# Attention scores QK^T on one core: two-bank PSUM tiles, copies shared by ScalarE and VectorE, and operands kept by half blocks

## The chip, the cores and the metric

The kernel runs on one core of one Trainium2 chip. The time of a kernel is the device time of one execution in microseconds, and several executions are summed up by their median. One more execution is taken by the hardware profiler; everything said about engines, waits and transfers comes from that one.

## What is computed

```python
def setup_inputs():
    batch, n_heads, seq, head_dim = 8, 12, 1024, 64
    return {
        "q": np.random.randn(batch, n_heads, seq, head_dim).astype(np.float32) * 0.1,
        "k": np.random.randn(batch, n_heads, seq, head_dim).astype(np.float32) * 0.1,
    }

def reference(q, k):
    return np.einsum('bhid,bhjd->bhij', q, k).astype(np.float32)
```

There are 96 independent heads. Each multiplies a 1024x64 matrix by the transpose of another one and gives 1024x1024 float32 scores, 4 MiB. All inputs together are 50.3 MB and the output is 402.7 MB.

## The kernel before

**Blocks.** The 96 heads are cut into blocks of 2, 2, 4 and then eleven blocks of 8 (`sizes`, line 33). A block's Q and K are loaded as float32 by one transfer each (`load`, line 70; the first two blocks head by head, line 82), cast to float16 by GpSimd, transposed so that the head dimension of 64 lies along the partitions, and multiplied by TensorE.

**From input to operand.** For all blocks but the first two, `cast_quads` (line 117) issues four GpSimd casts per half tile (line 131), each of 32 partitions by 1024 elements. `transpose_quads` (line 143) then has VectorE transpose 32x32 squares of a half tile (line 149). It writes with a gap: the view `"c (i r) -> c r i"` puts neighbouring elements of one square 64 elements, 128 bytes, apart for a block of 8. In return the result lies in the order of the rows of the head. A block's Q and K stay in one tile each of 4096 columns (`alloc`, line 139, two buffers). The first two blocks go through TensorE transposes instead (`transpose_rows`, line 151).

**Pairs.** In the blocks of 8, two heads share one pass over TensorE. `space` (line 194) spreads Q into one of two constant tiles, `spaced_even` and `spaced_odd`, of which every second column is zero for each half of the partitions (VectorE copies, line 200, two for a pair). `pair_scores` (line 208) then runs eight steps; each fills a PSUM tile of four banks (128x2048 float32) with four matmuls (line 219), and ScalarE copies the tile to the output tile `o_sb` in SBUF (line 226). Two PSUM tiles rotate. A pair's output tile is 128 partitions by 16384 float32, 8 MiB, and one transfer from the SP queue writes it to DRAM (line 233). Two output tiles rotate, so the copies into a tile wait for the transfer that last read it.

**Order.** Every instruction keeps program order on its engine (`pin`). Work for the next block is put between the steps of a pair by the dictionary `side`: after step 0 the `space` of the next pair, after step 1 the transposes of the next block, and in the third pair of a block, after steps 2 and 6, the two loads of the block after next (issued from ScalarE's queue, line 77). GpSimd's casts follow a queue of their own (`to_half`, line 274). The heads of the first three blocks are written singly, into halves of the two output tiles (`scores`, line 160); head 0 is copied in 1024-element pieces by ScalarE and VectorE in turn.

Of the kernel before, what the change touches and what calls it, by code (L numbers as in the profile page):

```python
# [13 lines left out]
def kernel(  # L14
# [11 lines left out]
    GMAX = 4  # L26
    assert D == 64 and NT == 8 and BH % (2 * GMAX) == 0

# [4 lines left out]
    sizes = [2, 2, 4] + [8] * ((BH - 8) // 8)  # L33
    assert sum(sizes) == BH
    PE_BLOCKS = 2
    NMAX = max(sizes)
    SINGLES = 3
    CHUNK = 32 * 32
# [8 lines left out]
    half_pool = ctx.enter_context(tc.tile_pool(name="half_pool", bufs=3))  # L47
    tr_pool = ctx.enter_context(tc.tile_pool(name="tr_pool", bufs=2))
    out_pool = ctx.enter_context(tc.tile_pool(name="out_pool", bufs=2))

    pin = tc.keep_in_program_order

    def half_tile():
        half_sb = half_pool.tile([P, CHUNK], F16, tag="half")
        return half_sb

    class Block:

        def __init__(self, first, N, by_pe):
            self.first, self.N, self.by_pe = first, N, by_pe
            self.R = N * S // P
            self.elems = self.R * D
            self.raw = [None] * 2
            self.rows = [None] * 2
            self.halves = {}
            self.cut = max(1, self.R * 32 // CHUNK + (self.R * 32 % CHUNK > 0))

        def load(self, x, eng):  # L70
            if self.raw[x] is None:
                x_sb = in_pool.tile([P, self.elems], F32, tag="x")
                self.raw[x] = x_sb
            start = self.first * S
            src = (qf, kf)[x][start : start + self.N * S]
            pin(
                eng.dma_start(
                    out=self.raw[x], in_=src.rearrange("(p r) d -> p (r d)", p=P)
                )
            )  # L80

        def load_head(self, n, x, eng):

            start = (self.first + n) * S
            src = (qf, kf)[x][start : start + S]
            m = S * D // P
            pin(
                eng.dma_start(
                    out=self.raw[x][:, n * m : (n + 1) * m],
                    in_=src.rearrange("(p r) d -> p (r d)", p=P),  # L90
                )
            )

        def cast_rows(self, x):
            n = S * D // P
            self.rows[x] = half_tile()[:, : 2 * n].rearrange(
                "p (r h d) -> p r h d", h=2, d=D
            )
            for half in range(2):
                pin(  # L100
                    nc.gpsimd.tensor_copy(  # L101
                        out=self.rows[x][:, :, half],
                        in_=self.raw[x][:, half * n : (half + 1) * n].rearrange(
                            "p (r d) -> p r d", d=D
                        ),
                    )
                )

        def chunks(self):
            return [  # L110
                (x, part, c)
                for x in range(2)
                for part in range(2)
                for c in range(self.cut)
            ]

        def cast_quads(self, x, part, c):

            m = self.R // self.cut
            half_sb = half_tile()[:, : m * 32]
            self.halves[x, part, c] = half_sb
            raw = self.raw[x].rearrange("p (r h d) -> p r h d", h=2, d=32)
            for half in range(2):
                b = 2 * half + part
                for h in range(2):
                    q0 = 32 * (2 * half + h)
                    pin(  # L130
                        nc.gpsimd.tensor_copy(  # L131
                            out=half_sb[q0 : q0 + 32].rearrange(
                                "p (r d) -> p r d", d=32
                            ),
                            in_=raw[32 * b : 32 * b + 32, c * m : (c + 1) * m, h],
                        )
                    )

        def alloc(self):
            self.qT = tr_pool.tile([P, NMAX * S // 2], F16, tag="qT")  # L140
            self.kT = tr_pool.tile([P, NMAX * S // 2], F16, tag="kT")

        def transpose_quads(self, x, part, c):
            src = self.halves[x, part, c].rearrange("p (r i) -> p r i", i=32)
            n, m = self.N * S // 4, self.R // self.cut
            dst = (self.qT, self.kT)[x][:, part * n : (part + 1) * n].rearrange(
                "c (i r) -> c r i", i=32
            )[:, c * m : (c + 1) * m]
            pin(nc.vector.transpose(out=dst, in_=src))  # L149

        def transpose_rows(self, x, ps_pool, copy):
            ps = ps_pool.tile([P, S], F32, tag="po")
            t_ps = ps.bitcast(F16)[:, : NT * P].rearrange("c (t m) -> c t m", m=P)
            for t in range(NT):
                pin(nc.tensor.transpose(t_ps[:, t], self.rows[x][:, t], ident))  # L155
            dst = (self.qT, self.kT)[x][:, :S].rearrange("c (m t) -> c m t", t=NT)
            src = t_ps.rearrange("c t m -> c m t")
            pin(copy(out=dst, in_=src))  # L158

        def scores(self, n, side, ps_pool, w, o_sb):  # L160

            half, g = divmod(n, self.N // 2)
            cs = slice(half * D, (half + 1) * D)

            qT = self.qT.rearrange("c (g m t) -> c g t m", t=NT, m=P)
            kT = self.kT.rearrange("c (g j) -> c g j", j=S)
            for u in range(NT // w):
                ps = ps_pool.tile([P, w * S], F32, tag="po")
                for tt in range(w):
                    for j in range(2):  # L170
                        js = slice(j * 512, (j + 1) * 512)
                        at = tt * S + j * 512
                        pin(
                            nc.tensor.matmul(  # L174
                                ps[:, at : at + 512],
                                qT[cs, g, w * u + tt],
                                kT[cs, g, js],
                            )
                        )
                dst = o_sb[:, w * u : w * u + w].rearrange("p t j -> p (t j)")  # L180
                if w == 1 and u % 2:
                    pin(nc.vector.tensor_copy(out=dst, in_=ps))  # L182
                else:
                    pin(nc.scalar.copy(out=dst, in_=ps))  # L184
                for do in side.get(u, []):
                    do()
# [7 lines left out]
        def space(self, g):  # L194

            sp = spaced[g % 2].rearrange("c t i s -> c i t s")
            for s in range(2):
                cs = slice(s * D, (s + 1) * D)
                pin(
                    nc.vector.tensor_copy(  # L200
                        out=sp[cs, :, :, s],
                        in_=self.qT[cs, g * S : (g + 1) * S].rearrange(
                            "c (i t) -> c i t", t=2 * NT
                        ),
                    )
                )

        def pair_scores(self, g, side, ps_pool):

            sp = spaced[g % 2].rearrange("c t i s -> c t (i s)")  # L210
            kT = self.kT[:, g * S : (g + 1) * S]
            o_sb = out_pool.tile([P, 2 * NT, S], F32, tag="out")
            for u in range(NT):
                ps = ps_pool.tile([P, 2 * S], F32, tag="po")
                for tt in range(2):
                    for j in range(2):
                        at = tt * S + j * 512
                        pin(
                            nc.tensor.matmul(  # L219
                                ps[:, at : at + 512],  # L220
                                sp[:, 2 * u + tt],
                                kT[:, j * 512 : j * 512 + 512],
                            )
                        )
                dst = o_sb[:, 2 * u : 2 * u + 2].rearrange("p t j -> p (t j)")
                pin(nc.scalar.copy(out=dst, in_=ps))  # L226
                for do in side.get(u, []):
                    do()
            heads = of[self.first : self.first + self.N].rearrange(
# [4 lines left out]
                    out=heads[g], in_=o_sb.rearrange("p t j -> p (t j)")  # L234
                )
            )

    blocks, first = [], 0
    for i, N in enumerate(sizes):
        blocks.append(Block(first, N, i < PE_BLOCKS))  # L240
        first += N
# [40 lines left out]
    for b in blocks[:PE_BLOCKS]:  # L282
        for x in range(2):
            b.cast_rows(x)
# [103 lines left out]
```

## Time and profile before

| what | value |
|---|---|
| runs | 1081.09, 1080.99, 1077.4 us, median 1080.99 |
| profiled execution, its own time | 1078.84 us |
| its span, first to last instruction | 1077.1 us |
| busy, share of the span | PE 47%, VectorE 62%, ScalarE 64%, GpSimd 43% |
| mean granted TensorE clock | 0.789 |
| DRAM read, written | 50.33 MB, 402.65 MB; 421 GB/s over the span |
| copies of a pair on ScalarE | 8 of 1880 ns |
| VectorE transpose of a half tile | 4852 ns |
| GpSimd cast | 1232 ns in the mean |

The page of the profile lists for each engine its busy time, then the span in forty slices, the DMA queues, the chain of work that ended last, and groups of equal instructions with the mean duration of one and what ended the idle time ahead of them. "L226" is line 226 of the kernel. DMA transfers all run on the same 16 DMA engines; a queue's share is the time of its packets over 16 engines' span. The trace behind the page keeps the start, the duration, the size and the queue of every DMA packet.

### The profile page before, as it was taken

The numbers are of one execution on the slowest core, as the hardware profiler recorded it, in microseconds if no ns is written. First come the engines' busy times: TensorE is split into PE (matmuls) and PEld (weight loads), VectorE is DVE, ScalarE is ACT, GpSimd is POOL, SyncE is SP. The second block draws the span as 40 slices with busy tenths as digits, with TensorE's granted clock in tenths as the row PEclk, the third lists the DMA queues.
The fourth block names the chain that finished last, engine by engine and source line by source line (L and its number), as shares of the span: only waits on it lengthen the run. The fifth ranks groups of instructions, "written<-read, shape, count | busy, mean of one in ns | idle before, by whom it ended". The sixth has DMA issues, their size and how long they took to land.

```text
span 1077.1 us, 4435 instructions
## 1 busy us (share of the span) xinstructions
PE 504.8 (47%) x1568; PEld 175.8 (16%) x1568; DVE 670.6 (62%) x187; ACT 690.1 (64%) x386; POOL 459.1 (43%) x384
## 2 busy tenths in 40 slices
PE   6873444543454445354345443544433644355550
PEld 2321111111111111111112111111111211111110
DVE  2999775586666676558665657656756656773100
ACT  4885566765686566576568656667556865587780
POOL 5899517515531831751553273175145418310000
PEclk9999777887678776788778877678866877778785
DMA  9999999999999999998999999999999899999998
GB/s 389 428 428 430 427 419 438 428 421 416 447 402 428 415 431 425 427 427 372 434 447 402 438 433 405 424 429 431 371 433 443 363 428 455 427 431 431 427 428 355
DMA packets 12118, 453.27 MB, mean 421 GB/s; under 512 B 1344, under 2 KB 1344, under 8 KB 2368
## 3 DMA queue, kind: packets, MB, share of 16 engines
q1 hardware_dynamic: 8352, 406.85, 88.3%
q10 hardware_dynamic: 3744, 46.14, 10.2%
q8 instruction: 12, 0.20, 0.1%
q14 instruction: 10, 0.08, 0.0%
HBM read 50.33 MB, written 402.65 MB: 421 GB/s over the span
## 4 chain that ended last, share of the span: by engine, by line
DMA 63%; ACT 26%; PE 7%; issue 1%; ACTq 0%; DVE 0%; POOL 0%; SPq 0%
DMA out_dram<-o_sb 57%; ACT o_sb L226 24%; PE ps L219 5%; DMA out_dram<-early 3%; DMA out_dram<-singles 2%; PE ps L174 2%; ACT singles L184 1%; ACT early L184 1%; DMA early<-in_q_dram 0%; PE ps L155 0%; ACTq L383 0%; POOL half_sb L101 0%; DVE kT L158 0%; DVE singles L182 0%; ACT kT L158 0%
## 5 line engine op out<-in xcount | busy, mean ns | idle before, releaser
L226 ACT COPY o_sb<-ps 128x2048 f32<-128x2048 f32 x352 | 632.6, 1880 | 338.2 <-DMA out_dram<-o_sb 309.6
L131 POOL CAST half_sb<-x_sb 32x1024 f16<-32x1024 f32 x352 | 433.7, 1232 | 471.9 <-DMA x_sb<-in_q_dram 236.9
L219 PE MATMUL ps<-kT,spaced_odd 128*128 128x512 f16 x704 | 222.2, 451 | 263.1 <-ACT o_sb L226 263.1
L219 PE MATMUL ps<-kT,spaced_even 128*128 128x512 f16 x704 | 220.6, 448 | 266.6 <-ACT o_sb L226 253.1
L200 DVE COPY spaced_odd<-qT 64x1024 f16<-64x1024 f16 x44 | 117.3, 2666 | 166.9 <-PE ps L219 166.2
L149 DVE STREAM_TRANSPOSE qT<-half_sb 128x1024 f16<-128x1024 f16 x46 | 214.4, 4852 | 1.6 <-POOL half_sb L131 0.9
L149 DVE STREAM_TRANSPOSE kT<-half_sb 128x1024 f16<-128x1024 f16 x46 | 214.3, 4854 | 0.6
L200 DVE COPY spaced_even<-qT 64x1024 f16<-64x1024 f16 x44 | 117.9, 2681 | 155.2 <-PE ps L219 154.5
L219 PEld LDWEIGHTS <-spaced_even 128*128 128x128 f16 x704 | 76.4, 109 | 411.1 <-issue 367.8
L219 PEld LDWEIGHTS <-spaced_odd 128*128 128x128 f16 x704 | 76.6, 109 | 408.7 <-issue 365.6
L174 PE MATMUL ps<-kT,qT 64*128 64x512 f16 x128 | 57.9, 620 | 8.3 <-ACT singles L184 3.0
L184 ACT COPY early<-ps 128x2048 f32<-128x2048 f32 x16 | 29.2, 1870 | 6.2 <-PE ps L174 5.9
L184 ACT COPY singles<-ps 128x2048 f32<-128x2048 f32 (+1 forms) x16 | 25.9, 1654 | 10.5 <-PE ps L174 8.8
L174 PEld LDWEIGHTS <-qT 64*128 64x128 f16 x128 | 19.6, 157 | 44.8 <-issue 40.5
L131 POOL CAST half_sb<-early 32x1024 f16<-32x1024 f32 x16 | 16.5, 1034 | 12.1 <-PE ps L155 6.3
L158 DVE COPY qT<-ps 128x1024 f16<-128x1024 f16 x2 | 2.4, 1224 | 12.3 <-PE ps L155 12.3
L182 DVE COPY singles<-ps 128x1024 f32<-128x1024 f32 x4 | 4.9, 1225 | 4.3 <-PE ps L174 4.3
L155 PE MATMUL ps<-ident,half_sb 128*128 128x128 f16 x32 | 4.1, 308 | 6.7 <-POOL half_sb L101 6.1
L101 POOL CAST half_sb<-early 128x512 f16<-128x512 f32 x8 | 4.6, 613 | 3.9 <-DMA early<-in_q_dram 3.9
L158 ACT ACT_TABLE_LOAD x1 | 1.3, 1283 | 5.8 <-DMA early<-in_q_dram 5.8
L155 PEld LDWEIGHTS <-half_sb 128*128 128x128 f16 x32 | 3.2, 139 | 8.6 <-POOL half_sb L101 6.4
L158 DVE COPY kT<-ps 128x1024 f16<-128x1024 f16 x1 | 1.2, 1225 | 4.3 <-PE ps L155 4.3
(9 smaller groups left out, 5.5 us busy)
## 6 DMA issues: line engine op xcount, KB each, us to landing
x_sb<-in_k_dram ACTq DMA_DIRECT2D x11, 2048.0 KB, 47.2
x_sb<-in_q_dram ACTq DMA_DIRECT2D x10, 2048.0 KB, 28.7
out_dram<-singles SPq DMA_DIRECT2D x4, 4096.0 KB, 19.6
out_dram<-early SPq DMA_DIRECT2D x4, 4096.0 KB, 25.0
x_sb<-in_q_dram SPq DMA_DIRECT2D x1, 2048.0 KB, 18.0
early<-in_q_dram SPq DMA_DIRECT2D x4, 256.0 KB, 4.6
early<-in_k_dram ACTq DMA_DIRECT2D x4, 256.0 KB, 5.0
early<-in_q_dram SPq DMA_DIRECT2D x1, 1024.0 KB, 9.1
```

Of the source, the lines that this page charges most:

```text
L101: nc.gpsimd.tensor_copy(out=self.rows[x][:, :, half], in_=self.raw[x][:, half * n : (half + 1) * n].rearrange("p (r d) -> p r d", d=D),)
L131: nc.gpsimd.tensor_copy(out=half_sb[q0 : q0 + 32].rearrange("p (r d) -> p r d", d=32), in_=raw[32 * b : 32 * b + 32, c * m : (c + 1) * m, h],)
L149: pin(nc.vector.transpose(out=dst, in_=src))
L155: pin(nc.tensor.transpose(t_ps[:, t], self.rows[x][:, t], ident))
L158: pin(copy(out=dst, in_=src))
L174: nc.tensor.matmul(ps[:, at : at + 512], qT[cs, g, w * u + tt], kT[cs, g, js],)
L182: pin(nc.vector.tensor_copy(out=dst, in_=ps))
L184: pin(nc.scalar.copy(out=dst, in_=ps))
L200: nc.vector.tensor_copy(out=sp[cs, :, :, s], in_=self.qT[cs, g * S : (g + 1) * S].rearrange("c (i t) -> c i t", t=2 * NT),)
L219: nc.tensor.matmul(ps[:, at : at + 512], sp[:, 2 * u + tt], kT[:, j * 512 : j * 512 + 512],)
L226: pin(nc.scalar.copy(out=dst, in_=ps))
```

## The change

- **PSUM.** One pool of four tiles of two banks (128x1024 float32) serves the whole kernel. A pair has sixteen steps of two matmuls and one copy. The copies of steps 1, 4, 7, 10 and 13 are VectorE's and the other eleven are ScalarE's.
- **Transposes.** In the blocks of 8 the VectorE transpose writes its output without gaps. For K the result goes to a new tile `step_sb`, and a further VectorE copy puts it in the order of the rows. For Q the order is left as it is, and `space` reads and writes other strides to make up for it.
- **Half blocks.** The unit of Q and K tiles is a `Part`, half a block of 8: two pairs. Its qT and kT have 2048 columns each, in three buffers each, where a whole block's had 4096 in two. Half tiles for the casts have four buffers instead of three.
- **Order.** All side work of a pair now follows step 13: in the first pair of a part the `space` of the second pair, and then three of the next part's four transposes (with one K copy); in the second pair the fourth transpose, its K copy and the next part's first `space`. The two loads of a block stand after steps 2 and 12 of the second pair of every second part, still on ScalarE's queue. GpSimd's casts of a part are written after the part three ahead of it.
- The first blocks are handled by a class of their own; heads 1 to 7 are copied by ScalarE alone in pieces of 1024 elements.

```diff
+    BY_VECTOR = (1, 4, 7, 10, 13)
...
-    half_pool = ctx.enter_context(tc.tile_pool(name="half_pool", bufs=3))
-    tr_pool = ctx.enter_context(tc.tile_pool(name="tr_pool", bufs=2))
+    half_pool = ctx.enter_context(tc.tile_pool(name="half_pool", bufs=4))
+    step_pool = ctx.enter_context(tc.tile_pool(name="step_pool", bufs=1))
+    q_pool = ctx.enter_context(tc.tile_pool(name="q_pool", bufs=3))
+    k_pool = ctx.enter_context(tc.tile_pool(name="k_pool", bufs=3))
     out_pool = ctx.enter_context(tc.tile_pool(name="out_pool", bufs=2))
+    po_pool = ctx.enter_context(
+        tc.tile_pool(name="po_pool", bufs=4, space=bass.MemoryType.PSUM)
+    )
...
+    def ps_tile():
+        ps = po_pool.tile([P, S], F32, tag="po")
+        return ps
+
+    def turned():
+        qT = q_pool.tile([P, 2 * S], F16, tag="qT")
+        kT = k_pool.tile([P, 2 * S], F16, tag="kT")
+        return qT, kT
+
+    def products(weights, kT, dst, copy):
+        ps = ps_tile()
+        for j in range(2):
+            at = slice(j * 512, j * 512 + 512)
+            pin(nc.tensor.matmul(ps[:, at], weights, kT[:, at]))
+        pin(copy(out=dst, in_=ps))
...
-        def transpose_quads(self, x, part, c):
-            src = self.halves[x, part, c].rearrange("p (r i) -> p r i", i=32)
-            n, m = self.N * S // 4, self.R // self.cut
-            dst = (self.qT, self.kT)[x][:, part * n : (part + 1) * n].rearrange(
-                "c (i r) -> c r i", i=32
-            )[:, c * m : (c + 1) * m]
-            pin(nc.vector.transpose(out=dst, in_=src))
...
+    class Part:
+        def __init__(self, number):
+            self.unit, self.part = divmod(number, 2)
...
+        def transpose(self, x, c):
+            if self.turned is None:
+                self.turned = turned()
+            src = self.halves[x, c].rearrange("p (r i) -> p r i", i=QUAD)
+            if x:
+                step_sb = step_pool.tile([P, S], F16, tag="step")
+                dst = step_sb
+            else:
+                dst = self.turned[0][:, c * S : (c + 1) * S]
+            pin(nc.vector.transpose(out=dst.rearrange("c (r i) -> c r i", i=QUAD), in_=src))
+            if x:
+                kT = self.turned[1].rearrange("c (i a r) -> c a i r", a=CUT, r=ROWS)
+                pin(
+                    nc.vector.tensor_copy(
+                        out=kT[:, c], in_=step_sb.rearrange("c (r i) -> c i r", i=QUAD)
+                    )
+                )
...
         def space(self, g):
-            sp = spaced[g % 2].rearrange("c t i s -> c i t s")
+            sp = spaced[g].rearrange("c t (i a) s -> c a t i s", a=4)
             for s in range(2):
                 cs = slice(s * D, (s + 1) * D)
...
+                qT = self.turned[0][cs].rearrange("c (a t g i) -> c g a t i", a=4, t=2 * NT, g=2)
+                pin(nc.vector.tensor_copy(out=sp[cs, :, :, :, s], in_=qT[:, g]))
...
+        def scores(self, g, side):
+            sp = spaced[g].rearrange("c t i s -> c t (i s)")
+            kT = self.turned[1][:, g * S : (g + 1) * S]
             o_sb = out_pool.tile([P, 2 * NT, S], F32, tag="out")
...
+            for t in range(2 * NT):
+                copy = nc.vector.tensor_copy if t in BY_VECTOR else nc.scalar.copy
+                products(sp[:, t], kT, o_sb[:, t], copy)
+                for do in side.get(t, []):
                     do()
...
+    for number, part in enumerate(parts):
+        for g in range(2):
+            side = {13: []}
+            if g:
+                side[13].append(lambda: do_for(number + 1, "transpose", 1, 1))
+                side[13].append(lambda: do_for(number + 1, "space", 0))
+            else:
+                side[13].append(lambda: part.space(1))
+                for x, c in ((0, 0), (0, 1), (1, 0)):
+                    side[13].append(lambda x=x, c=c: do_for(number + 1, "transpose", x, c))
+            if number == g == 0:
+                side[2] = [lambda: load(3, nc.scalar)]
+            if number % 2 and g:
+                unit = number // 2
+                side[2] = [lambda: load(2 * (unit + 2), nc.scalar)]
+                side[12] = [lambda: load(2 * (unit + 2) + 1, nc.scalar)]
+            part.scores(g, side)
+        if number == 0:
+            do_for(2, "cast")
+        do_for(number + 3, "cast")
```

The instructions that issue transfers are the same in number, size and shape in both kernels: 44 outputs of a pair, 8 of a head, and the same loads.

## The prediction

> **What bounds the kernel now.** I read the DMA rows of the page first, then the chain of work, the groups, the waits, and the timeline of one unit of four pairs.
>
> ```profile
> DMA  9999999999999999998999999999999899999998
> ...
> DMA packets 12118, 453.27 MB, mean 421 GB/s; under 512 B 1344, under 2 KB 1344, under 8 KB 2368
> ...
> q1 hardware_dynamic: 8352, 406.85, 88.3%
> q10 hardware_dynamic: 3744, 46.14, 10.2%
> ```
>
> The DMA engines are busy in every slice from the first to the last. q1 (SP) and q10 (ScalarE's queue) take 98.5% of 16 engines' span, which leaves 16 us of idle time per engine in the mean. Some 2 us ahead of the first input packet and about as much at the end belong to it.
>
> ```profile
> DMA 63%; ACT 26%; PE 7%; issue 1%; ACTq 0%; DVE 0%; POOL 0%; SPq 0%
> ...
> L226 ACT COPY o_sb<-ps 128x2048 f32<-128x2048 f32 x352 | 632.6, 1880 | 338.2 <-DMA out_dram<-o_sb 309.6
> L131 POOL CAST half_sb<-x_sb 32x1024 f16<-32x1024 f32 x352 | 433.7, 1232 | 471.9 <-DMA x_sb<-in_q_dram 236.9
> ...
> L200 DVE COPY spaced_odd<-qT 64x1024 f16<-64x1024 f16 x44 | 117.3, 2666 | 166.9 <-PE ps L219 166.2
> L149 DVE STREAM_TRANSPOSE qT<-half_sb 128x1024 f16<-128x1024 f16 x46 | 214.4, 4852 | 1.6 <-POOL half_sb L131 0.9
> ...
> L182 DVE COPY singles<-ps 128x1024 f32<-128x1024 f32 x4 | 4.9, 1225 | 4.3 <-PE ps L174 4.3
> ...
> L158 DVE COPY kT<-ps 128x1024 f16<-128x1024 f16 x1 | 1.2, 1225 | 4.3 <-PE ps L155 4.3
> ```
>
> ScalarE, 26% of the chain, looks like a second bound. Its row says otherwise: of 338.2 us idle ahead of its copies, 309.6 end with the transfer that frees an output tile. The waits and the timeline of a load-free stretch show how little it lacks:
>
> ```profile
> ACT o_sb L226 <- DMA out_dram<-o_sb: 309.6, 42, 11.8
> ```
> ```profile
> 202.92 3.63 ACT L226 COPY o_sb<-ps 128x2048 f32<-128x2048 f32 x2 [6.88 <-DMA out_dram<-o_sb]
> ...
> 217.75 19.57 SPq L233 DMA_DIRECT2D out_dram<-o_sb  x2
> ...
> 222.22 3.63 ACT L226 COPY o_sb<-ps 128x2048 f32<-128x2048 f32 x2 [4.50 <-DMA out_dram<-o_sb]
> ...
> 226.11 0.34 ACTq L77 DMA_DIRECT2D x_sb<-in_q_dram  x1
> ```
>
> A fill of an output tile takes 217.75 - 202.92 = 14.8 us; between two tiles coming free lie 222.22 - 202.92 = 19.3 us. About 1.3 us pass from issue to first packets, so 19.3 - 14.8 - 1.3 = 3.2 us are spare.
>
> The packet records say more. Each output transfer is closed by sixteen 4-byte packets, one per DMA engine. In most transfers most of the sixteen lie within half a microsecond and one comes 2.7 to 7.4 us later. The forerunners run dry about once per unit: added up, dips of 0.3 to 1.6 us make 12 us of the span. The last engine does not. From the closing packet at 113.5 us to the one at 1075.6 us its packets follow each other without a hole, and a load-free transfer costs it 19.32 us, eight packets of 2.418. **That one engine's work is the bound**, and an earlier output transfer only lengthens its queue.
>
> **The change, part by part.** The sum stands on the profiled execution: span 1077.1, own time 1078.84 us (1.7 around the span), 2.2 below the median 1080.99.
>
> *Transfers.* Sizes and counts do not change: 0. VectorE and ScalarE get some 380 more instructions; the instruction queue's packets of 8 KB cost 0.31 us, and 0.28 MB for 4435 instructions makes 63 bytes each, so three more packets, at most 0.9 us if all fall on the last engine.
>
> *Copies of a pair.* Removed: 8 x 1.88 = 15.0 us on ScalarE. Added: 11 on ScalarE at 1.01 us (head 0's copies of this shape in the timeline; 11.1 us) beside 5 on VectorE at 1.225 (L182; 6.1 us). TensorE needs 0.94 us per two matmuls after idle time (1.88 per four in the chain) and 0.51 later (four in 1.02); four tiles wait ready in either kernel. Stepping through sixteen tiles by these rows gives 11.5 us for a fill, the fifth VectorE copy ending at 9.2. That is 3.3 us earlier than 14.8. The dips of the forerunners shrink; the last engine gains 0.
>
> *Transposes.* Four per two pairs write without gaps. Not in the trace; bounds are 4.85 (L149, same operation, 128-byte steps) and 1.22 us (L158, same elements, dense writes). I take 1.22: the two transpose rows differ from it by nothing but the gap and the kind of operation, and `space`, no transpose, pays 2.67 for wide steps too. The Trainium skill, "VectorE: DVE Perf Modes", section "The three transpose paths", has 311 ns for 128x128, an estimate of 1.2 to 1.3 us for 1024 columns; no run here shows it yet.
>
> *K copy.* Two per two pairs, new, reading with 64-byte steps and writing runs of 32. Bounds: 1.22 (L158 reads PSUM with wide steps at no extra cost) and 4.85. I take 2.67, L200's: same engine, SBUF to SBUF, 1024 float16. The Trainium skill, "SBUF — State Buffer", section "Door 1: The DMA port swizzle", says each access that crosses to a new 16-byte line pays; by it the gapless transpose gets cheap, and this copy and `space`, still stepping by a line, do not. The trace agrees on L200's 2.67; with 1.22 for K the sum would be the same.
>
> *Space.* Now 16-byte write steps: 2.67 kept (2.45 alone in the timeline), bounds 1.22 and 4.85.
>
> VectorE per two pairs: before 4 x 4.85 + 4 x 2.67 = 30.1 us; after 4 x 1.22 + 2 x 2.67 + 4 x 2.67 + 10 x 1.225 = 33.2, against 2 x 22.2 us (a unit of four pairs takes 89). It does not bound by load. By order: in a part's first pair step 13 ends at 9.2, then 5.3 (`space`) + 3.7 (three transposes) + 2.7 = 20.9, 1.6 us after the next tile comes free, so that pair's first VectorE copy is late and its fill becomes some 13 us. In the second pair 9.2 + 3.9 + 5.3 = 18.4, plus 0.94 for a first tile: 19.3, just in time. A fill may grow to 19.3 - 1.8 = 17.5 us before the last engine starves. Cover: 4.5 us. Cost 0.
>
> *Loads.* ScalarE now meets two waits in the second pair of every second part, ahead of its remaining copies. Load one needs two half tiles cast (4.3 to 4.9 us each by L131) behind the previous pair's transposes: cast by 5.6 us into the fill, reached at 2.1, 3.5 us lost. Load two needs a half tile freed only by this pair's transpose after step 13: copy to 12.8, transpose to 14.0, four casts to 18.6; ScalarE arrived at 13. Two copies are queued behind it. The fill becomes 21 us, and the SP queue waits for it. That does not starve the DMA engines while load packets are pending: in the packet records this window lasts 23.6 us on the last engine, and load two alone brings it 8 x 0.61 = 4.9 us of work. If that cover fails, each microsecond too much costs 11 us. Cost taken: 0.
>
> *Start.* Head 1's output is issued some 3 us sooner (no change of PSUM pool), heads 1 to 7 take 8 x 1.01 = 8.1 us, below the 9.7 us that 4 MiB take. Dips near 22 us, 0.1 to 0.6: -0.6. Heads stay behind the transfers: 0.
>
> Sum: 1077.1 + 0.3 - 0.6 = 1076.8, with 1.7 around it 1078.5. On a median I give 1078, 0.3% below 1080.99: no change by the 0.5% that a measurement of this kernel can tell (the three runs alone spread by 0.34%).
>
> **The rivals.**
>
> *The late engine is not late by nature (faster).* From 113.5 to 1075.6 us the last engine spent 23 us more than its full-speed packets (44 x 19.34 + 144 load packets x 0.61), the mean engine 13.7 over the whole run. Its slow packets, about 1 us each, come where the others change transfers during loads. With other timing this may go, and with it the forerunners' 12 us. For it: fill times drop below the skew. Against it: load-free transfers show no slow packets and still no recovery. Worth up to 23 - 13 = 10 us: 1068.
>
> *ScalarE's wait for the second load starves the engines (slower).* Against it the pending load packets; for it, no slack in the 23.6 us window: 21 + 1.8 = 22.8. It decides from 0.8 us on; at casts of 4.9 and transposes of 1.5 us the fill is 22.5, 1.5 us too long in eleven units: 1078 + 17 = 1095.
>
> *VectorE's chain between pairs gets too long (slower).* The period of two pairs is at least 9.2 + 9.2 + 2 x 5.3 + 0.9 us plus four transposes and two K copies; in 44.4 us the latter may take 14.5, and 12.7 where the first load's wait holds up step 13 by 3.6 in every second two. I expect 4 x 1.22 + 2 x 2.67 = 10.2. It decides from a K copy of 3.9 us on, or a transpose of 1.85. For it: a copy that gets only one port's rate would cost like L149's 4.85; then 14.6, 1.9 over, 22 times: 1120. Were transposes still at 4.85, so that writing without gaps did not do what it says, it would be 24.7, 12 over: 1340. Against it: the dense rows at 1.22.
>
> **How the numbers follow.** Forecast (transfers bound as before) 0.45; late engine recovers 0.25; load wait 0.18; VectorE's chain 0.12, nearly all of it at K's price. The forecast's own range is 1073 to 1083. The range 1066 to 1100 takes in the first rival whole and the load wait, and leaves out most of VectorE's chain and the tails. Faster than 1075.6: 0.29, most of the first rival and a part of the forecast; slower than 1086.4: 0.29; between: 0.42.
>
> **What would show it.** Right: DMA slices as full as before; ScalarE's wait for output transfers longer than 309.6 us, with copies of 1.01; transposes near 1.2; closing packets of load-free transfers still 19.32 apart on the last engine. The load step: a wait of ScalarE for GpSimd (line 85 there) of 3 and 5 us in eleven pairs. Wrong: holes in the last engine's packets; VectorE copies of step 1 ended late by K copies above 3.9 us or transposes above 1.85; or a last engine no later than the rest, and a span near 1066.

## The result, and the profile after

| kernel | median us | lowest to highest, runs | ratio to before, 95% interval |
|---|---|---|---|
| before | 1079.04 | 1073.87 to 1081.72, 20 | |
| after | 1081.72 | 1080.15 to 1084.49, 20 | 1.0027 [1.0016, 1.0038] |

The change costs 2.7 us, a quarter of a per cent: less than the 0.5% that was named as "no change", but the interval leaves out no change at all. The profiled execution of the changed kernel took 1080.31 us, with a span of 1078.5; the one of before took 1078.84, with 1077.1. So the two traces differ by 1.4 us, about half of what the medians differ by.

The DMA rows of the changed kernel (in the queue rows: packets, MB, share of 16 engines' span):

```profile
DMA  9999999999999999999899999999999999999998
...
DMA packets 12122, 453.30 MB, mean 420 GB/s; under 512 B 1344, under 2 KB 1344, under 8 KB 2368
...
q1 hardware_dynamic: 8352, 406.85, 87.3%
q10 hardware_dynamic: 3744, 46.14, 11.3%
```

The transfers still fill the span, with four packets more than before. But q1, the outputs, takes 1.0% less of it, and q10, nearly all loads, takes 1.1% more. The bytes are the same, so the load packets got slower and the output packets faster.

The chain that ended last and the groups of the changed kernel (count, busy us and mean ns of one, then idle time before them and what ended it):

```profile
DMA 48%; PE 17%; DVE 14%; ACT 10%; POOL 5%; issue 2%; ACTq 0%; SPq 0%; DVEq 0%
...
L85 POOL CAST half_sb<-x_sb 32x1024 f16<-32x1024 f32 x352 | 484.9, 1378 | 460.7 <-DVE qT L208 338.0
L76 ACT COPY o_sb<-ps 128x1024 f32<-128x1024 f32 x484 | 453.5, 1041 | 519.0 <-DMA out_dram<-o_sb 326.6
L76 DVE COPY o_sb<-ps 128x1024 f32<-128x1024 f32 x220 | 269.4, 1224 | 317.1 <-PE ps L75 197.4
...
L222 DVE COPY spaced_even<-qT 64x1024 f16<-64x1024 f16 x44 | 140.2, 3187 | 0.3
L222 DVE COPY spaced_odd<-qT 64x1024 f16<-64x1024 f16 x44 | 107.0, 2431 | 1.0
L212 DVE COPY kT<-step_sb 128x1024 f16<-128x1024 f16 x44 | 62.5, 1420 | 1.6
...
L208 DVE STREAM_TRANSPOSE step_sb<-half_sb 128x1024 f16<-128x1024 f16 x44 | 53.7, 1220 | 3.9 <-POOL half_sb L85 3.9
L208 DVE STREAM_TRANSPOSE qT<-half_sb 128x1024 f16<-128x1024 f16 x44 | 52.3, 1227 | 0.7
```

The new operations came out as small as hoped or smaller: transposes 1.22 us, the K copy 1.42. Yet the chain's share of DMA fell from 63% to 48%, and VectorE and GpSimd now stand in it with 14% and 5%: there are places where transfers wait for them. The waits show where:

```profile
ACT o_sb L76 <- DMA out_dram<-o_sb: 326.6, 30, 15.5
...
ACT o_sb L76 <- POOL half_sb L85: 127.2, 17, 11.4
```

ScalarE has a new wait of 127.2 us in all, for GpSimd. The timeline of ScalarE, from a load-free pair to the pair that issues two loads and the one behind it (start, duration, and the idle time ahead with what ended it):

```profile
201.49 4.89 ACT L76 COPY o_sb<-ps 128x1024 f32<-128x1024 f32 x5 [14.70 <-DMA out_dram<-o_sb]
207.01 5.73 ACT L76 COPY o_sb<-ps 128x1024 f32<-128x1024 f32 x6 [0.63 <-PE ps L75]
...
240.99 1.93 ACT L76 COPY o_sb<-ps 128x1024 f32<-128x1024 f32 x2 [8.52 <-DMA out_dram<-o_sb]
246.29 0.34 ACTq L177 DMA_DIRECT2D x_sb<-in_q_dram  x1
246.66 6.51 ACT L76 COPY o_sb<-ps 128x1024 f32<-128x1024 f32 x7 [3.75 <-POOL half_sb L85]
263.35 0.33 ACTq L177 DMA_DIRECT2D x_sb<-in_k_dram  x1
263.72 12.27 ACT L76 COPY o_sb<-ps 128x1024 f32<-128x1024 f32 x13 [10.55 <-POOL half_sb L85]
291.28 4.89 ACT L76 COPY o_sb<-ps 128x1024 f32<-128x1024 f32 x5 [15.30 <-DMA out_dram<-o_sb]
```

A load-free fill takes 212.74 - 201.49 = 11.25 us. In the load pair two waits stand inside the fill, 3.75 and 10.55 us. Two of the thirteen copies behind the second wait end this fill, the other eleven are the next pair's; so it takes 24.7 us, from 240.99 to about 265.7. VectorE and GpSimd in that stretch tell why the second wait is so long:

```profile
252.68 1.24 DVE L208 STREAM_TRANSPOSE step_sb<-half_sb 128x1024 f16<-128x1024 f16 x1
253.95 1.02 DVE L212 COPY kT<-step_sb 128x1024 f16<-128x1024 f16 x1
254.88 6.46 DVE L222 COPY spaced_even<-qT 64x1024 f16<-64x1024 f16 x2
```
```profile
253.98 9.33 POOL L85 CAST half_sb<-x_sb 32x1024 f16<-32x1024 f32 x4 [3.40 <-DVE step_sb L208]
```

The four casts that the load waits for run beside the two `space` copies, and each holds up the other. The casts take 9.33 us (the fastest one of the run 1.03), the copies 6.46, where the same pair of copies took 4.88 without casts beside it. The Trainium skill, "SBUF — State Buffer", section "Who interferes with whom", says that GpSimd has no ports to SBUF of its own but shares VectorE's second pair, held by one of the two at a time. These numbers agree with it.

The packet records show what this did to the transfers. A record names the queue of a packet and not its engine; "the last engine" is the one whose closing packet comes last. In each unit of four pairs nearly all DMA engines run dry once, for 0.9 to 1.8 us in the mean, between the end of the first load and the first packets of the second. The last engine goes over to the second load without a hole in seven of nine units. The second load runs for some 5.5 us with no output transfer beside it. About a third of its packets are slow, by 0.1 to 1.4 us, and two thirds of that time are lost while it is alone. On the other side the late engine of before is hardly late any more. The table has the run from the 14th transfer of SP's queue on, the output of the last head (means over the 16 engines; "extra" is time above a packet's full-speed duration; the lag is from the first to the last of a transfer's sixteen closing packets; lag and unit are taken over the nine units with loads):

| | idle us | extra, outputs us | extra, loads us | lag, median (max) us | one unit on the last engine us |
|---|---|---|---|---|---|
| before | 11.8 | 11.5 | 1.1 | 4.33 (7.44) | 89.73 |
| after | 11.4 | 1.0 | 13.8 | 1.68 (2.70) | 90.03 |

So two large effects nearly cancel in the means: 10.5 us gained on output packets, 12.7 lost on load packets. The last engine's closing packets show where the 1.4 us between the two traces lie: the 14th transfer closes 1.6 us sooner after the change (111.87 against 113.50 us), the nine units with loads take 9 x 0.30 = 2.7 us longer, and the load-free transfers at the end 0.3 us longer.

### The profile page after: what moved, and what is told of

It is laid out like the page before. It is cut to its first block, busy times and chain, and to the rows that moved or that the text cites. A ratio compares the mean times of both kernels' runs of the same rounds, so it can differ in the third digit from the quotient of the medians.

```text
span 1078.5 us, 4965 instructions
## 1 busy us (share of the span) xinstructions
PE 542.9 (50%) x1568; PEld 188.9 (18%) x1568; DVE 706.4 (65%) x451; ACT 511.6 (47%) x546; POOL 510.4 (47%) x384
## 4 chain that ended last, share of the span: by engine, by line
DMA 48%; PE 17%; DVE 14%; ACT 10%; POOL 5%; issue 2%; ACTq 0%; SPq 0%; DVEq 0%
DMA out_dram<-o_sb 42%; PE ps L75 17%; ACT o_sb L76 10%; DVE spaced_even L222 6%; POOL half_sb L85 5%; DMA out_dram<-early 3%; DMA out_dram<-singles 2%; DVE o_sb L76 2%; DVE spaced_odd L222 2%; DVE step_sb L208 2%; DVE kT L212 1%; DVE qT L208 0%; DMA early<-in_q_dram 0%; PE ps L131 0%; ACT singles L76 0%
## 5 line engine op out<-in xcount | busy, mean ns | idle before, releaser
L85 POOL CAST half_sb<-x_sb 32x1024 f16<-32x1024 f32 x352 | 484.9, 1378 | 460.7 <-DVE qT L208 338.0
L76 ACT COPY o_sb<-ps 128x1024 f32<-128x1024 f32 x484 | 453.5, 1041 | 519.0 <-DMA out_dram<-o_sb 326.6
L76 DVE COPY o_sb<-ps 128x1024 f32<-128x1024 f32 x220 | 269.4, 1224 | 317.1 <-PE ps L75 197.4
L75 PE MATMUL ps<-kT,spaced_odd 128*128 128x512 f16 x704 | 257.1, 530 | 265.8 <-ACT o_sb L76 135.6
L212 DVE COPY kT<-step_sb 128x1024 f16<-128x1024 f16 x44 | 62.5, 1420 | 1.6
L208 DVE STREAM_TRANSPOSE step_sb<-half_sb 128x1024 f16<-128x1024 f16 x44 | 53.7, 1220 | 3.9 <-POOL half_sb L85 3.9
L208 DVE STREAM_TRANSPOSE qT<-half_sb 128x1024 f16<-128x1024 f16 x44 | 52.3, 1227 | 0.7
L76 ACT COPY early<-ps 128x1024 f32<-128x1024 f32 x32 | 30.0, 1150 | 8.5 <-POOL half_sb L85 6.3
L76 ACT COPY singles<-ps 128x1024 f32<-128x1024 f32 x28 | 26.5, 1190 | 4.2 <-PE ps L75 4.2
L143 DVE STREAM_TRANSPOSE kT<-half_sb 128x1024 f16<-128x1024 f16 x2 | 9.8, 4908 | 0.0
L143 DVE STREAM_TRANSPOSE qT<-half_sb 128x1024 f16<-128x1024 f16 x2 | 9.6, 4793 | 0.0
## 6 DMA issues: line engine op xcount, KB each, us to landing
x_sb<-in_q_dram ACTq DMA_DIRECT2D x10, 2048.0 KB, 19.4
x_sb<-in_q_dram SPq DMA_DIRECT2D x1, 2048.0 KB, 19.6
early<-in_q_dram SPq DMA_DIRECT2D x1, 1024.0 KB, 10.3
```

What stands on the lines that cost most here:

```text
L75: pin(nc.tensor.matmul(ps[:, at], weights, kT[:, at]))
L76: pin(copy(out=dst, in_=ps))
L85: nc.gpsimd.tensor_copy(out=half_sb[to : to + QUAD].rearrange("p (r d) -> p r d", d=32), in_=raw[b : b + QUAD, rows, h],)
L143: nc.vector.transpose(out=dst.rearrange("c (i r) -> c r i", i=QUAD), in_=self.halves[x, part].rearrange("p (r i) -> p r i", i=QUAD),)
L208: pin(nc.vector.transpose(out=dst.rearrange("c (r i) -> c r i", i=QUAD), in_=src))
L212: nc.vector.tensor_copy(out=kT[:, c], in_=step_sb.rearrange("c (r i) -> c i r", i=QUAD))
```

## The experiments

The first theory was that ScalarE's wait for GpSimd is the cost: without it the late engine's recovery would remain as a gain. The rival was that the transfers, not the wait, set the time.

**Six half tiles instead of four**, so that no cast waits for a transpose of the same pair.

```diff
-    half_pool = ctx.enter_context(tc.tile_pool(name="half_pool", bufs=4))
+    half_pool = ctx.enter_context(tc.tile_pool(name="half_pool", bufs=6))
```

> The changed kernel with six half tiles for the casts instead of four, so that both loads of a unit find their casts done and ScalarE no longer waits for GpSimd (3.75 and 10.55 us in the load pair of the changed kernel's timeline). Theory A, the late fill of the load pair is what costs: ScalarE's waits for GpSimd at the loads go from 127 us to under 15, the load pair's fill from 25 us to 12 or 13, the dips of 1.2 us per unit vanish, and the load packets, no longer alone on the DMA engines, lose their 14.7 us per engine of extra time: 1082 - 11 - 3 = 1066 to 1071. Theory B, loads cost their extra time wherever they lie: beside output packets they slow these as in the kernel before (11.5 us per engine, and one engine 4 us behind the rest): only the dips go or are replaced, 1076 to 1081.

Measured: 1095.84 us (1083.99 to 1096.98, 6 runs), ratio 1.0140 [1.0096, 1.0184]. The wait is gone; the largest waits of ScalarE are now

```profile
ACT o_sb L76 <- DMA out_dram<-o_sb: 464.8, 41, 16.1
ACT o_sb L76 <- PE ps L75: 42.0, 45, 8.9
```

and the kernel is 14 us slower. ScalarE gained 127 us and waits for the transfers instead. The lag grew to 9.94 us (at most 12.38), the output packets' extra to 15.4, the idle time to 22.2 us. The closing packets of a unit on the last engine are 25.8, 27.2, 19.9 and 19.3 us apart, where the changed kernel has 22.4, 28.1, 20.1 and 19.3: the loss lies in the first of the two transfers beside the loads, which takes 3.4 us longer; the second takes 0.9 us less.

**Second load moved to the next pair**, behind its step 4, with the casts in that order.

```diff
-                side[12] = [lambda: load(2 * (unit + 2) + 1, nc.scalar)]
+            if number and number % 2 == 0 and not g:
+                late = 2 * (number // 2 + 1) + 1
+                side[4] = [lambda: load(late, nc.scalar)]
```

> The changed kernel with the second load of a unit issued after step 4 of the next pair instead of step 12 of this one; four half tiles as in the changed kernel. Only the wait of 10.55 us goes, that of 3.75 stays. Theory A: load pair's fill some 15 us, no dip, 1066 to 1072. Theory B: 1076 to 1081, with the slow packets among the output packets again. If e1 is fast and this one is not, the first load's wait counts too.

Measured: 1083.5 us (1074.09 to 1086.66, 12 runs), 1.0041 [1.0018, 1.0064].

```profile
ACT o_sb L76 <- DMA out_dram<-o_sb: 437.9, 40, 16.8
...
ACT o_sb L76 <- POOL half_sb L85: 29.8, 9, 3.9
```

ScalarE's wait for GpSimd fell by 97 us and its wait for the transfers rose by 111. The load packets' extra fell from 13.8 to 6.0, the output packets' rose from 1.0 to 11.1, and the lag to 9.00. With these two runs the theory fell: take the wait away and the lag and the slow output packets come back.

**No loads for the later blocks**, in both kernels (the edit of the changed one is shown).

```diff
+        if unit >= 2:
+            raws[unit, x] = raws[1, x]
+            return
```

> The changed kernel without the loads of units 2 to 10 (casts read unit 1's inputs again, so the later heads are not those of the reference). 144 load packets of 0.611 us per engine go, 88.0 us at full speed. If the loads cost no more than that: 1081.7 - 88 = 994. Theory A and B both: the extra time (14.7 us on load packets, 11 us of dips, over eleven units; nine of them here) goes as well: 1081.7 - 88 - 20 = 973 to 977. Every transfer then takes 19.32 us from closing packet to closing packet.

> The kernel before without the loads of units 2 to 10 (the same inputs are left out, the later heads are not those of the reference). At full speed 1079.0 - 88 = 991. If the last engine's 23 us of extra time and its lag come from the loads, as read from the packet records: 1079 - 88 - 19 = 970 to 976, the same as the changed kernel without loads within 3 us. If the lag is a slow engine's nature and not the loads', it stays above 985.

Measured: 976.92 us after the change (976.75 to 976.99, 4 runs), 974.77 before it (974.71 to 974.82, 4 runs). So the change costs 2.15 us where there are no loads and hence no waits for them. What the loads add is nearly the same: 1081.72 - 976.92 = 104.8 us and 1079.04 - 974.77 = 104.3 us, against 18 x 8 x 0.611 = 88.0 us of full-speed load packets. The load-free transfers, which were to cost 19.32 us on the last engine throughout, do so only at first. In the changed kernel they cost 19.5 to 19.6 from the third transfer of 8 MiB on, in the kernel before 19.54 to 19.56 from about the tenth. In a later transfer most of the packets at the last engine's pace took up to 0.07 us longer than 2.418. These slow steps belong to the kernels without loads. In the traces of the two kernels with loads nearly every load-free transfer costs the last engine 19.32 us to the end, before the change and after it. So the 2.15 us are not seen as a part of the 2.7: there the longer time lies in the units with loads.

The next theory: fast fills have the next output already queued, so fifteen engines run ahead, and the last one meets the loads while it is behind. Slower fills should then help.

**Six half tiles with slower fills**: two copies by VectorE, and none.

```diff
-    BY_VECTOR = (1, 4, 7, 10, 13)
+    BY_VECTOR = (5, 10)
```
```diff
-    BY_VECTOR = (1, 4, 7, 10, 13)
+    BY_VECTOR = ()
```

> The kernel with six half tiles (1095.8 us) with two of a pair's sixteen copies on VectorE instead of five: a fill takes 14 x 1.01 to 1.04, some 14.5 us instead of 11.5. Theory C: one DMA engine lags the other fifteen, and while loads are in flight its output packets cost more the further the others run ahead; how far they can run ahead is what a fill leaves of 19.3 us. Then slower copies make the kernel faster: spread of the closing packets from 7 to 12 us down to 3 to 5, load-free steps of the last engine 19.32 as before, its slow packets fewer, 1096 down to 1076 to 1083. Theory D: the fill is not the cause, but something else of the six half tiles (casts or transposes at other times, loads early in the fill): 1090 or more.

> The kernel with six half tiles with all sixteen copies on ScalarE, a fill of 16.2 to 16.6 us. Theory C: spread at most 2 us, 1066 to 1078, the fastest of the row, unless the last engine itself starves (16.6 + 1.8 = 18.4 against 19.3). Theory D: 1090 or more. Theory of the prediction as it stood (the last engine's work is fixed): no change, 1094 to 1097.

Measured: 1082.18 us (1076.53 to 1090.44, 12 runs), 1.0020 [0.9996, 1.0044], and 1083.48 (1082.0 to 1086.14, 12 runs), 1.0045 [1.0027, 1.0063]. A load-free fill took 12.9 and 14.8 us, where it takes 11.1 with five copies by VectorE; 14.5 and 16.2 to 16.6 had been expected. Copying more slowly makes the kernel with six half tiles 12 to 14 us faster, and the lag falls from 9.94 to 6.49 and 4.15 us (the profiled execution with two copies was the slowest of its twelve, 1090.4 us). The direction is right. The slower of the two fills brought nothing more, and 1066 to 1078 us had been expected of it, so the lag alone does not give the time.

**The kernel before with each copy cut in two**, meant to make its fill 1.5 us longer, and **the changed kernel with ScalarE alone copying**.

```diff
-                dst = o_sb[:, 2 * u : 2 * u + 2].rearrange("p t j -> p (t j)")
-                pin(nc.scalar.copy(out=dst, in_=ps))
+                for tt in range(2):
+                    pin(nc.scalar.copy(out=o_sb[:, 2 * u + tt], in_=ps[:, tt * S : (tt + 1) * S]))
```
```diff
-    BY_VECTOR = (1, 4, 7, 10, 13)
+    BY_VECTOR = ()
```

> The kernel before with each ScalarE copy of 2048 elements cut into two of 1024, nothing else: the fill goes from 14.8 to some 16.3 us, and ScalarE's busy time up by 50 us. Theory C: the others can run ahead by 1.5 us less, the spread of 3.7 to 5 us falls to 2 to 3.5, and the kernel gets faster: 1068 to 1076 against 1078 or 1079. If the dips of the other fifteen engines were a loss, as one would read them: slower by 1.5 us per load-free transfer in eleven units or more, 1090 to 1100.

> The changed kernel (four half tiles) with all sixteen copies on ScalarE. In its load pair the two waits of 3.75 and 10.55 us are added to a longer fill: 25 + 4 = 29 us, and the DMA engines run dry some 4 us longer per unit. Theory C: spread is already 0.8 to 2.7 us here, so nothing is to be gained from a slower fill, and the load pair costs 11 x 3 to 4 us: 1105 to 1125. If the load pair's lateness is covered by the loads as the prediction had it: 1080 to 1084.

Measured: 1079.02 us (1072.32 to 1085.71, 12 runs), 0.9991 [0.9966, 1.0017], and 1083.75 (1078.26 to 1085.72, 12 runs), 1.0041 [1.0021, 1.0061]. The first run did not test what it was made for: sixteen copies of 1024 elements took 14.97 us against 14.8, so the fill was hardly longer, and the time stayed. What a longer fill would do to the kernel before is open. The changed kernel is at most some 2 us slower without VectorE's copies, and the intervals of the two ratios overlap. That is far less than expected, because its fill was not longer in the load pair but shorter: 14.8 us instead of 24.7. ScalarE no longer waits for GpSimd in the pairs (its only long wait is 310.8 us for output transfers, about the 309.6 of before), and the sums look like those of before: output packets 12.2 extra, loads 0.8, lag 4.11. So with four half tiles the way the copies are shared decides which of the two losses the kernel has, and hardly how long it takes.

The last theory: what costs is that the loads run beside the outputs, in a queue of their own. **Put the loads into the queue of the outputs**, SP's, ahead of an output transfer. This edit stands on the kernel with the second load moved.

```diff
-                side[2] = [lambda: load(2 * (unit + 2), nc.scalar)]
+                side[15] = [lambda: load(2 * (unit + 2), nc.sync)]
...
-                side[4] = [lambda: load(late, nc.scalar)]
+                side[15] = [lambda: load(late, nc.sync)]
```

> The changed kernel with each unit's two loads issued from the SP queue, just ahead of the output transfers of the load pair and of the pair behind it, instead of from ScalarE's queue. A load then lies in the same rings between two output transfers, neither beside them nor alone behind a wait. Theory E: what costs is either loads beside outputs (slow output packets on the engine that lags, 11 to 15 us) or a drained queue and loads alone (11 us idle and 14 us on load packets, the changed kernel); in ring order neither arises: spread under 3 us, idle time under 3 us, out and load packets together under 8 us too long, 1064 to 1070. Rival: reads cost their 13 to 15 us of extra time wherever they run: 1076 to 1081.

Measured: **1065.94 us** (1065.1 to 1068.3, 5 runs), 0.9885 [0.9858, 0.9911].

```profile
DMA  9999999999999999999999999999999999999996
...
q1 hardware_dynamic: 10944, 444.60, 97.3%
q10 hardware_dynamic: 1152, 8.39, 1.9%
```
```profile
ACT o_sb L76 <- DMA out_dram<-o_sb: 456.9, 42, 14.5
```

The same bytes and the same engines, but now each engine takes the load's packets in turn, between those of two outputs. From the second to the sixth of these loads the closing packets on the last engine are 19.4 to 19.6 us apart for an output and 4.87 for a load, which is eight full-speed packets of 0.61; later a load there takes 5.4 to 7.0 us, and an output beside it less in return. The engines idle 0.7 us in the mean from the last head's output on. Loads now cost 1065.94 - 976.92 = 89.0 us, 1.0 above their full-speed packets. Of ScalarE's waits in the pairs nearly all are for outputs. The lag is not gone (about 5 us, where under 3 had been expected), so a lag of this size goes with a fast kernel. The queue and the place of the loads were changed together; which of the two does it, or whether both are needed, is not shown.

**The same in the kernel before**, loads ahead of the third and fourth pair's outputs, and **the same with six half tiles**.

```diff
-            if g == pairs // 2:
-                side[2].append(lambda: next_load(nc.scalar))
-                side[6].append(lambda: next_load(nc.scalar))
+            if g >= pairs // 2:
+                side[7].append(lambda: next_load(nc.sync))
```
```diff
-    half_pool = ctx.enter_context(tc.tile_pool(name="half_pool", bufs=4))
+    half_pool = ctx.enter_context(tc.tile_pool(name="half_pool", bufs=6))
```

> The kernel before with its two loads of a block on the SP queue, ahead of the output transfers of the third and the fourth pair, instead of on ScalarE's queue in the third pair; nothing else. Theory E: the lag of one engine no longer grows at the loads, the last engine's 23 us of extra time shrink to some 10: 1064 to 1070. Rival: 1076 to 1081.

> The kernel with six half tiles (1095.8 us with loads on ScalarE's queue) with its loads on the SP queue as in the other two. Theory E: with loads in ring order the early fills do no harm any more, 1064 to 1070, some 27 us less than with the same fills and loads beside the outputs. Rival, fills that end early are harmful in themselves: 1085 or more.

Measured: 1074.5 us (1072.87 to 1076.17, 12 runs), 0.9964 [0.9948, 0.9979], and 1065.91 (1065.51 to 1067.61, 5 runs), 0.9882 [0.9853, 0.9911]. Six half tiles, which cost 14 us with the loads beside the outputs, cost nothing with the loads in order. The kernel before gains only 4.5 us, less than expected. One of its two loads still takes 6.5 to 6.8 us on the last engine in most units, the other 4.9, and about 2 us of idle time remain.

**No loads, and ScalarE alone copying**, to see whether the fast fill causes the 2.15 us of the load-free part.

```diff
-    BY_VECTOR = (1, 4, 7, 10, 13)
+    BY_VECTOR = ()
```

> The changed kernel without the loads of its later blocks, as in the run before it with loads left out (the data of an early block is used again, so the scores of later heads are not the reference's), and with ScalarE alone copying: 16 copies of about 1.01 us, a fill of some 17 us, which is longer than the 14.8 us of the kernel before and still shorter than the 19.32 us of a transfer. Without loads the change cost 2.15 us: 976.92 against 974.77 us, nearly all of it in load-free transfers that cost the last DMA engine 19.6 instead of 19.32 us, from the 15th transfer on after the change and from the 22nd on before it. Theory that the speed of the fills does this (a next transfer that already waits lets the other engines change over at once, while the last one is still at its old transfer): the fill is later, so the slow steps begin later or are smaller, and the time is 973 to 975.5 us. Rival, that it is not the fill but what else changed (more instructions, the first blocks, where the tiles lie): 976 to 978 us, with steps of 19.6 from about the 15th transfer on.

Measured: 976.37 us (one run; the executions of one kernel without loads lie within 0.25 us of each other). The sixteen copies took 14.76 us, not the 17 expected; that is the fill of before, and the lag fell from 6.11 to 3.19, that of before as well. But the steps of 19.6 us begin with the third transfer of 8 MiB again, and stay. So 0.55 of the 2.15 us may be the fill; the rest is not, and its cause is open.

## Why the prediction was right or wrong

The forecast was 1078 with a range of 1073 to 1083 of its own, "no change", with the transfers as the bound. The time, 1081.7, lies inside that range, but it went up by 0.27% where the sum had it 0.3% down. That it lies so near is in part luck: two effects of more than 10 us that the sum left out nearly cancel.

- **Transfers bound: right.** The DMA slices are as full as before, and load-free transfers still close 19.32 us apart on the last engine, the sign that was named. **"Sizes and counts do not change: 0" and the last engine's fixed work: wrong.** The counts held (four packets more), the durations did not. What the last engine spends on one unit ranges from 88.3 us (loads in the queue of the outputs) to 91.9 (six half tiles), with the same packets to move; from before to after it rose from 89.73 to 90.03.
- **Copies of a pair: right.** 1.04 us each on ScalarE in the mean (1.01 taken), fills of 11.25 us against 11.5, and the wait for outputs longer than before, 326.6 us. That the faster fill gains nothing is right too. What was missing is that it can lose: with six half tiles it costs 12 to 14 us.
- **Transposes: right**, 1.22 us, the lower bound. The estimate of 1.2 to 1.3 us that the prediction drew from the 311 ns for 128x128 in the Trainium skill, "VectorE: DVE Perf Modes", section "The three transpose paths", agrees with it. Eight times 311 ns would be 2.49 us, so the estimate supposes a fixed part in the 311 ns; no run here separates one.
- **K copy: too large**, 2.67 taken, 1.42 measured and 1.02 alone, below the lower bound of 1.22. The rule of the 16-byte line, quoted from the Trainium skill, "SBUF — State Buffer", had this copy pay for its reads at 64-byte steps as `space` does for its writes. Here the wide reads cost far less than the wide writes: `space` takes 2.43 us at 16-byte steps, more than twice as much. Whether the reads cost anything is not shown, since no run has such a copy with dense reads.
- **Space: 2.67 taken, 2.81 in the mean**, from 2.43 (odd, mostly alone) to 3.19 (even, beside casts). The difference was not foreseen. What makes it, the casts beside `space`, also lengthened the load wait.
- **VectorE's chain between pairs: right.** From step 13 to the next fill it takes 241.0 - 230.7 = 10.3 us instead of 11.7, and its first copy of that fill starts at 241.01, as the output tile comes free (ScalarE's starts at 240.99). The third rival did not come.
- **Loads, "Cost taken: 0": the step that failed.** The first wait was right, 3.75 us against 3.5. The second was 10.55 instead of 5.6, since the four casts were priced at 4.3 to 4.9 us by the rows of before, and took 9.33 beside `space`. So the fill takes 24.7 us, not 21, and the cover named, pending load packets, ends before it: on most engines the first load is through before the packets of the second come. Nearly all engines idle for 0.9 to 1.8 us per unit, and the second load starts alone on slow packets: 12.7 us lost in the mean. Against it stand the 10.5 us gained on output packets, which the sum had at "the last engine gains 0". On the last engine, which the prediction took for the bound, the balance is a loss of 0.30 us per unit, 2.7 us in nine units.
- **The rivals.** The first and the second both came, and nearly cancel. The late engine did recover (lag 4.33 to 1.68, output packets 10.5 us faster), as the first had it. ScalarE's wait did starve the engines, as the second had it, at less than its price of 17 us. The rivals had been treated as alternatives. The runs fit one cause for both: a late fill lets the last engine catch up while the others wait. In the three runs that take the long wait away (six half tiles, the second load moved, ScalarE alone copying) the lag is back at 4.1 to 9.9 us and the output packets' extra at 11 to 15 us.
- **Start: -0.6 taken**; on the last engine the last head's output closed 1.6 us sooner after the change, on the other engines no sooner (111.78 against 111.55 us for the last but one).

That the time rose, and did not fall, lies by the traces in the units with loads (+2.7 us on the last engine), which outweigh the sooner start. That is one execution of each kernel, and a balance of gains and losses of more than 10 us each; no run shows why it comes out as a loss. Open stay three causes more: why load packets are slow when they start alone, why packets of a late engine get slower beside loads, and why without loads the last engine's packets are a few hundredths of a microsecond longer from some transfer on.

## What to carry to other kernels

In a kernel bound by its transfers, look at what each DMA engine does at the changes between transfers, not only at the mean busy share. A wait that is taken away, or a fill made faster, can cost time there (1095.8 us here), and a new wait can nearly pay for itself. Where reads and writes compete, try the reads in the queue of the writes, in the order in which they are to run: the changed kernel with both loads on SP's queue beats both kernels, 1065.9 us against 1079.0 and 1081.7.

## What the runs showed of the hardware

- Against the same kernel without loads, the loads cost 104 to 105 us in both kernels, which issue them from ScalarE's queue beside or between the outputs. In SP's queue ahead of an output they cost 89.0 us in the changed kernel and 99.7 in the kernel before (1074.5 - 974.8). The Trainium skill, "DMA: Bandwidth & Descriptors", section "Issuing engines are not separate DMA queues", says that all issuing engines' transfers interleave on the same 16 engines, and that issuing from several saves only issue time. Here more hung on it: 17.6 us (1083.5 against 1065.9), where queue and place in the order were changed together.
- The sixteen DMA engines finish a transfer with one up to 12.4 us later than the first. The lag does not give the time: about 5 us go with the fastest kernel, 4.3 with one 13 us slower. At the end of the run, where no transfer follows, the engines that are done stand idle for it: the closing packets of the fastest kernel's last transfer lie 6.2 us apart, those of the changed kernel 2.0.
- Of VectorE's copies from float16 to float16 in SBUF, one that writes at 16-byte steps took 2.43 us (64x1024), and one that reads at 64-byte steps and writes runs of 32 took 1.02 us (128x1024), each without a GpSimd cast beside it.
